# Who writes the low halves of the weights, where the convolution reads, who copies the S5 carries, and how rows are spread

## The chip, the cores and the metric

The kernel runs on one core of one Trainium2 chip. The metric is the device time of one launch in microseconds. The core has five engines with a queue each: PE (TensorE, with its weight loads shown as PEld), DVE (VectorE), ACT (ScalarE), POOL (GpSimd) and SP (SyncE, which here only starts DMAs). Each engine takes its instructions strictly in the order in which they stand in its queue and waits on semaphores for the others.

## The reference, cut to what matters

One inference step of a hybrid recurrent layer for 2,048 prompt tokens, 16 meta tokens and 8 short sample sequences of 8 tokens. All is float32.

```
h = rms_norm(x); proj = h @ w_in                      # 1024 -> 8,720 columns
A: q,k,v = silu(causal_conv4(qkv)); gated delta rule  # DeltaNet, 4 heads of 128
B: mLSTM with exponential gates                       # 4 heads of 128
C: S5: h[t] = lam*h[t-1] + B u[t], y = Re(C h) + d*u  # 32 groups, 64 complex states, then GLU
x = x + (sum_b sigmoid(gate_b) * (branch_b @ w_b)) @ w_out;  y = rms_norm(x)
```

`causal_conv4` is a convolution over the last four tokens with four taps per feature. Its input is the projected column block itself, and the last three columns of one stretch of tokens are carried to the next.

## The kernel before, in words

The tokens are cut into six blocks of 336, 384, 384, 384, 384 and 256 columns (`BLOCKS`; the first also holds the samples and the meta tokens). Activations lie feature-major: 128 features on the partitions, tokens along the row. A dense product (`product`) makes 128 output features for all tokens of a block and sums over 8 or 4 slices of 128 input features into one bank of PSUM, called `pd`; there are three such banks. Because PE gets its operands as rounded halves, every slice takes three matmuls: high weights by high activations, high weights by low activations, low weights by high activations.

The weights of four slices form a piece of 128x512 floats (`weights`): SP loads it (`w`), ACT casts it to the high half (`wh`), and a subtraction `w - wh` makes the low half (`wl`). A block needs 182 pieces and the program 1,092. The subtraction is given to DVE or to POOL by count: every second piece goes to POOL (`WPOOL = 2`), in the first block every fourth (`WPOOL0 = 4`). There are three buffers of `wh` and three of `wl`, so the halves of a piece can be written only when PE has finished the piece three earlier. A piece is 12 matmuls.

In each block the steps are issued in this order: `rows` (the per-token gates, a long chain of small DVE operations), `columns` (transposes of these rows on PE and exponentials), four S5 projections and four S5 scans (`s5_scan`), then the projections of q, k, v for DeltaNet (`dn_proj`) and mLSTM (`ml_proj`) and the recurrences and outputs by the list `PLAN`. A scheduler turns that order, with priorities, into the order of each engine's queue; the loads, casts and subtractions of weights have a higher priority (`WPRIO`) than what is issued around them. So the order is written nowhere by hand.

`dn_proj` copies the product from `pd` to a buffer `raw` in SBUF (ACT), puts the three carried columns in front of it (POOL), multiplies by the last tap (ACT, `cacc`), adds the three other taps on DVE from shifted views of `raw`, and saves the last three columns (POOL, buffer `cbuf`). `s5_scan` copies the carried state of four columns into the scan's first column (DVE), scans with DVE, combines with DVE and POOL, and copies the state at the end out again (DVE). `spread` brings a row of the gates into all partitions by a matmul of 32 rows of ones with 32 rows of `rx`; `rx` has three such groups of 32 rows.

Most arithmetic goes through helpers, so that in the profile L185 is any `tensor_tensor`, L193 any `scalar_tensor_tensor`, L196 any matmul, L179 a copy, L182 an activation, and the tiles tell which is which.

Of the kernel before, what the change touches and what calls it, by code (L numbers as in the profile page):

```python
# [17 lines left out]
D = 1024  # L18
# [9 lines left out]
# Prompt tiles of 128 tokens per block; the first block also has the tile of samples and meta tokens.  # L28
# [7 lines left out]
WPOOL, WPOOL0 = 2, 4  # L36
WB = (4, 3, 3)
UNITS = 12
# Order of the steps of the first block and of the others: projections of q, k, v (d, m), recurrences, outputs.
PLAN0 = ("m8 m7 R m6 m10 m1 m0 m9 m2 m4 m5 d4 m3 d5 m11 M d0 d3 d2 S d7 d8 d9 d10 d1 d6 pre inv d11 N X1 D "  # L40
         "F X2 Ud E X0 Um").split()
PLAN = ("d0 d1 m1 m0 m2 m3 d6 d2 d10 d3 m4 m7 m6 d7 d4 d5 m5 d8 pre d9 m9 d11 m11 m10 m8 M F N inv D X2 "
        "X1 E X0").split()

# Buffers of temporaries: floats of a partition, and how many.
# [17 lines left out]
# Column blocks of the input projection, in the order in which the host lays them out.  # L63
CB_S5U, CB_DN, CB_ML, CB_MLO, CB_MLZ, CB_S5Z, CB_DNZ, CB_GATE = 0, 4, 16, 28, 32, 36, 40, 44

# Columns of the array of vectors.
V_NW, V_TAP, V_BG, V_DNN, V_MLN, V_S5D, V_BGLU, V_FN, V_RB, V_AL, V_LDT, V_LR, V_LI, NV = (
    0, 8, 56, 80, 81, 82, 86, 90, 98, 99, 100, 116, 132, 148)
# Columns of the array of constants.
# [34 lines left out]
class Kernel:  # L104
# [36 lines left out]
    def temp(self, shape, tag, dt=F32):  # L141
        """A tile of a set of buffers that several steps share."""
# [14 lines left out]
    def pair(self, w, name):  # L157
        """Two tiles of the four heads, the second of width w, in one unit."""
        u = self.unit([P, 4 * P + 4 * w], name=name)
        return u[:, 0:4 * P].rearrange("p (h n) -> p h n", h=4), u[:, 4 * P:].rearrange("p (h n) -> p h n", h=4)  # L160
# [41 lines left out]
    def rsqrt(self, out, x, shape, also_sqrt=None):  # L202
        """out = 1/sqrt(x) on a small tile of positive floats: a first guess from their bits, three Newton steps."""
# [13 lines left out]
    def weights(self, src, k0):  # L217
# [3 lines left out]
        with self.tc.high_priority(offset=WPRIO if self.wn > 1 else 5500):  # L221
            self.nc.sync.dma_start(w, src[:, k0:k0 + 4])
            self.A.copy(h, w)  # L223
            self.wn += 1
            pool = WPOOL if self.b else WPOOL0
            self.tt(self.G if pool and self.wn % pool == 0 else self.V, l, w, h, OP.subtract)
        return h, l

    def product(self, src, nk, xh, xl, T):
        t = self.pd.tile([P, 512], F32, name=self.name("pd"), tag="pd")  # L230
        o = t[:, :T]
        for k in range(nk):
# [4 lines left out]
            self.mm(o, l[:, k % 4], xh(k), start=False, stop=k == nk - 1)  # L237
        return o

    def proj(self, cb):  # L240
        return self.product(self.I["wi"][cb], 8, lambda k: self.xh[k // 4][:, k % 4, :],
                            lambda k: self.xl[k // 4][:, k % 4, :], self.T)

# [1 line left out]
    def setup(self):  # L245
# [14 lines left out]
        self.G.memset(self.ones, 1.0)  # L260
        self.halfv = self.const([P, NV])
        self.ts(self.V, self.halfv, self.vec, 0.5, OP.mult)
        c = self.small([P, 8], "setup")
        # the row groups' bias with its sign, and the rows' factor of softplus
# [19 lines left out]
    def block(self, b):  # L284
# [20 lines left out]
        # (first column, sequences, their length): chunks over which decays are summed  # L305
        self.segs = ([(0, 8, 8), (NS, 1, NM)] if self.first else []) + [(self.p0, BLOCKS[b], P)]

    def norm(self):
        """xn^T = x^T * norm_w * rstd, as two exact halves."""
# [12 lines left out]
        if self.first:  # L322
            # x^T * norm_w in halves, for the products that need not wait for rstd
# [37 lines left out]
    def rstd_row(self, acc):  # L361
        """1/rms of every token, in every partition of a row, from squares summed over k."""
# [16 lines left out]
    def bc(self, src, c0, ns, L, p0, p1, at):  # L379
        """[p, ns, L]: of each sequence its column `at`, repeated."""  # L380
# [6 lines left out]
    def rows(self):  # L387
# [11 lines left out]
        # softplus(u) = max(u, 0) + 2 artanh(e / (2 + e)), e = exp(-|u|)  # L399
# [17 lines left out]
        # cumulative sums by chunk: G in rows 0.., b in rows 32..  # L417
# [10 lines left out]
        # running maximum; M[:, 1 + t] is m after token t, M[:, 0] the block's first m  # L428
# [26 lines left out]
        # rows that go to all partitions: G; b - m; b + m(chunk start) - m  # L455
# [12 lines left out]
        # rows that become columns: G, G_last - G | ig - b, its state weight, -m | beta  # L468
# [1046 lines left out]
```

## Time and profile before

| what | value |
|---|---|
| time, median of 3 runs | 2888.38 us (2888.12 to 2891.21) |
| span of the profiled execution | 2881.7 us |
| what lies around that span, by the median | 6.7 us |
| PE, matmuls | 2695.2 us, 94% |
| DVE | 2005.7 us, 70% |
| POOL | 1463.6 us, 51% |
| ACT | 1237.3 us, 43% |

The profile is of one execution; its own total time is not listed apart from its span, so that 6.7 us of start and end are taken as the difference to the median. Busy times are sums over the whole span. A stage in which PE is busy all the time is set by PE; in the other stages one looks at what PE waits for. The granted clock is the share of full speed that TensorE's clock had in a stretch.

### The profile page before, as it was taken

Reading aid. Unit: us, or ns where it says so; the run is one execution under the profiler, and the core shown is the slowest. Engines: PE = TensorE matmul, PEld = TensorE weight load, DVE = VectorE, ACT = ScalarE, POOL = GpSimd, SP = SyncE. Lnnn points to the kernel's source line nnn. Section 1 sums busy time; section 2 is a strip of 40 time slices with the busy share of each in tenths; the row PEclk is TensorE's granted clock in tenths of the full one; section 3 lists DMA queues with packets and bytes.
Section 4 is the critical chain, followed back from the end, with each engine's and each line's share of the span. In section 5 each row is a group of like instructions: output and inputs, shape, how many; then the busy total and the mean of one; then the engine's idle time right before and its main releaser. Section 6 shows DMA issues by size and latency. Waiting matters only on the chain.

```text
span 2881.7 us, 49911 instructions
## 1 busy us (share of the span) xinstructions
PE 2695.2 (94%) x17416; PEld 2585.0 (90%) x17416; DVE 2005.7 (70%) x4030; ACT 1237.3 (43%) x2639; POOL 1463.6 (51%) x1545
## 2 busy tenths in 40 slices
PE   6898999998999999999998999999999999989897
PEld 5798888887999989899998989999989999978897
DVE  8789756789753488884458888345988734688854
ACT  4353334434533443443453453345335334444444
POOL 8853444355434545543464553445455345455555
PEclk9999999999999999999999999999999999998999
DMA  5544547544333455433345533345543434564544
GB/s 154 162 152 147 154 149 219 171 154 126 98 112 107 149 168 159 121 110 105 112 155 166 163 103 119 99 122 164 168 147 102 122 98 135 159 192 124 152 144 151
DMA packets 303292, 404.26 MB, mean 140 GB/s; under 512 B 109472, under 2 KB 138912, under 8 KB 303040
## 3 DMA queue, kind: packets, MB, share of 16 engines
q1 hardware_dynamic: 283248, 374.73, 43.0%
q10 hardware_dynamic: 19792, 26.34, 2.7%
q8 instruction: 137, 2.24, 0.3%
q14 instruction: 115, 0.94, 0.1%
HBM read 369.42 MB, written 31.53 MB: 139 GB/s over the span
## 4 chain that ended last, share of the span: by engine, by line
PE 40%; DVE 16%; issue 3%; DMA 3%; ACT 2%; POOL 1%; SPq 0%; DVEq 0%; ACTq 0%; POOLq 0%
PE pd L196 32%; PE pr L196 5%; DVE wl L185 2%; DVE cacc L193 2%; DVE s5a L1196 2%; PE s L196 1%; DVE invT L185 1%; DVE s5a L185 1%; DVE invU L185 1%; PE pr L200 1%; ACT wh L223 1%; DMA ox<-in_xt_dram 1%; DVE h L193 1%; POOL wl L185 1%; DVE nacc L185 1%
## 5 line engine op out<-in xcount | busy, mean ns | idle before, releaser
L185 POOL TENSOR_TENSOR wl<-w,wh 128x512 fp32r<-128x512 f32 x500 | 690.2, 1381 | 882.2 <-ACT wh L223 789.4
L196 PE MATMUL pd<-xh,wl 128*128 128x384 f32 (+2 forms) x3272 | 1083.9, 332 | 57.8 <-DVE wl L185 49.1
L223 ACT CAST wh<-w 128x512 fp32r<-128x512 f32 x1092 | 672.8, 618 | 1059.8 <-PE pd L196 742.1
L196 PE MATMUL pd<-xh,wh 128*128 128x384 f32 (+2 forms) x3272 | 1079.1, 330 | 6.5 <-ACT wh L223 5.3
L196 PE MATMUL pd<-xl,wh 128*128 128x384 f32 (+2 forms) x3272 | 1076.8, 329 | 3.5 <-DVE xl L185 3.5
L185 DVE TENSOR_TENSOR wl<-w,wh 128x512 fp32r<-128x512 f32 x592 | 469.8, 794 | 361.3 <-ACT wh L223 335.3
L196 PEld LDWEIGHTS pd<-xh,wl 128*128 128x128 f32 x3272 | 625.8, 192 | 84.0 <-DVE wl L185 63.5
L196 PEld LDWEIGHTS pd<-xh,wh 128*128 128x128 f32 x3272 | 627.9, 192 | 13.0 <-ACT wh L223 7.2
L196 PEld LDWEIGHTS pd<-xl,wh 128*128 128x128 f32 x3272 | 627.3, 192 | 9.0 <-DVE xl L185 4.7
L193 DVE SCALAR_TENSOR_TENSOR cacc<-raw,c,cacc 128x384 f32<-128x384 f32 (+2 forms) x252 | 171.0, 694 | 4.6 <-ACT cacc L182 2.5
L185 POOL TENSOR_TENSOR macc<-macc,mt 128x384 f32<-128x384 f32 (+2 forms) x96 | 106.2, 1107 | 56.8 <-DVE mt L193 54.9
L196 PE MATMUL pd<-mh,wl 128*128 128x384 f32 (+2 forms) x384 | 125.3, 329 | 5.3 <-POOL wl L185 4.2
L196 PE MATMUL pd<-mh,wh 128*128 128x384 f32 (+2 forms) x384 | 125.9, 330 | 3.6 <-DVE h L193 3.2
L196 PE MATMUL pd<-ml,wh 128*128 128x384 f32 (+2 forms) x384 | 124.4, 326 | 0.0
L193 DVE SCALAR_TENSOR_TENSOR mt<-mt,pd 128x384 f32<-128x384 f32 (+2 forms) x96 | 50.0, 521 | 96.3 <-PE pd L196 94.5
L185 POOL TENSOR_TENSOR s5a<-s5a,s5a 128x384 f32<-128x384 f32 (+2 forms) x72 | 82.6, 1156 | 66.5 <-DVE s5a L185 60.7
L185 DVE TENSOR_TENSOR invT<-invP,invU 48x31 f32<-48x31 f32 (+25 forms) x186 | 100.4, 540 | 10.4 <-DMA invP<-scrp 6.3
L1196 DVE TENSOR_TENSOR_SCAN s5a<-s5R,s5a,s5a 128x96 f32<-128x96 f32 (+2 forms) x192 | 97.5, 566 | 2.8 <-POOL s5a L185 2.7
L182 ACT ACTIVATE raw<-cacc 128x384 f32<-128x384 f32 (+2 forms) x72 | 35.9, 499 | 147.5 <-DVE cacc L193 136.5
L185 POOL TENSOR_TENSOR s5a<-s5a,s5t 128x384 f32<-128x384 f32 (+2 forms) x48 | 66.5, 1386 | 45.8 <-DVE s5a L1196 27.7
L196 PE MATMUL s<-s5U,s5w 128*128 128x96 f32 (+2 forms) x576 | 85.5, 278 | 3.4 <-DMA s5U<-us 2.3
L185 DVE TENSOR_TENSOR nacc<-nacc,nsq 128x384 f32<-128x384 f32 (+2 forms) x84 | 68.5, 816 | 28.4 <-ACT nsq L182 26.5
(396 smaller groups left out, 4744.5 us busy)
## 6 DMA issues: line engine op xcount, KB each, us to landing
w<-in_wi_dram SPq DMA_DIRECT2D x816, 256.0 KB
w<-in_wb_dram SPq DMA_DIRECT2D x144, 256.0 KB
s5w<-s5w SPq DMA_DIRECT2D x120, 256.0 KB
w<-in_wo_dram SPq DMA_DIRECT2D x96, 256.0 KB
s5t<-s5p SPq DMA_DIRECT2D x48, 192.0 KB
w<-in_wg_dram SPq DMA_DIRECT2D x24, 256.0 KB
xt<-in_xt_dram SPq DMA_DIRECT2D x32, 192.0 KB
ox<-in_xt_dram ACTq DMA_DIRECT2D x32, 192.0 KB
```

What stands on the lines that cost most here:

```text
L182: return self.A.activation(out, in_, f, **k)
L185: return eng.tensor_tensor(out, a, b, op=op)
L193: return self.V.scalar_tensor_tensor(out, a, s, b, op0=op0, op1=op1)
L196: return self.E.matmul(out, lhsT, rhs, start=start, stop=stop, **k)
L200: return self.E.transpose(out, in_, self.ident[:n, :n])
L223: self.A.copy(h, w)
L1196: V.tensor_tensor_scan(g[:, a, 1:1 + m], self.s5R[:, 4 * f + a:4 * f + a + 1].to_broadcast([P, m]), x[:, a, 0:m], g[:, a, 0:1], OP.mult, O ...
```

## The change

Four edits. All 1,092 subtractions go to DVE. In all blocks but the first the convolution reads the product in its bank of PSUM: the product is put 16 columns to the right, ACT writes the three carried columns just in front of it, and DVE's three taps read shifted views of the bank; the buffer `raw` then only takes the tanh. ACT also saves the last three columns, in all blocks. The six small copies of each S5 scan go from DVE to ACT. `spread` uses 96 rows of `rx` with a selector that is one in one group of 32 rows and zero elsewhere. The names `u0` to `s3` in `PLAN` issue the S5 steps in the place where they stood before.

```diff
 def weights(self, src, k0):
     ...
             self.wn += 1
-            pool = WPOOL if self.b else WPOOL0
-            self.tt(self.G if pool and self.wn % pool == 0 else self.V, l, w, h, OP.subtract)
+            self.tt(self.V, l, w, h, OP.subtract)
-    def product(self, src, nk, xh, xl, T):
+    def product(self, src, nk, xh, xl, T, lead=None):
         t = self.pd.tile([P, 512], F32, name=self.name("pd"), tag="pd")
         o = t[:, :T]
+        if lead is not None:
+            o = t[:, 16:16 + T]
     ...
+        if lead is not None:
+
+            self.A.copy(t[:, 13:16], lead)
+            self.lead = t
         return o
 def setup(self):
     ...
+        self.sel = self.const([P, 4], F32R, name="sel")
+        t = self.sel.bitcast(F32)
+        self.G.memset(t, 0.0)
+        for g in range(3):
+            self.G.memset(t[32 * g:32 * g + 32, g:g + 1], 1.0)
 def spread(self, i, g):
     ...
-        self.mm(p, self.onesr[32 * g:32 * g + 32], self.rx[32 * g:32 * g + 32, i, 0:4 * n])
+        self.mm(p, self.sel[0:96, g:g + 1].to_broadcast([96, P]), self.rx[0:96, i, 0:4 * n])
 def dn_proj(self, n):
     ...
-        ps = self.proj(CB_DN + n)
+        ps = self.proj(CB_DN + n, None if self.first else self.cbuf[b % 2][:, n])
     ...
+            self.A.copy(raw[:, so + 3:so + 3 + T - NS], ps[:, NS:T])
+            parts.append((acc[:, NS:T], lambda j: raw[:, so + j:so + j + T - NS]))
         else:
-            self.copy(self.G, raw[:, 0:3], self.cbuf[b % 2][:, n])
-        p1 = NS if self.first else 0
-        self.A.copy(raw[:, so + 3:so + 3 + T - p1], ps[:, p1:T])
-        parts.append((acc[:, p1:T], lambda j: raw[:, so + j:so + j + T - p1]))
-        self.copy(self.G, self.cbuf[(b + 1) % 2][:, n], raw[:, so + T - p1:so + T - p1 + 3])
+            parts.append((acc[:, :T], lambda j, t=self.lead: t[:, 13 + j:13 + j + T]))
+        self.A.copy(self.cbuf[(b + 1) % 2][:, n], ps[:, T - 3:T])
 def s5_scan(self, f):
     ...
-            self.copy(V, g[:, :, 0:1], car[:, j, ps4][:, :, None])
+            A.copy(g[:, :, 0:1], car[:, j, ps4][:, :, None])
     ...
-            self.copy(V, t[:, :, c0:c0 + 1], car[:, j, ps4][:, :, None])
+            A.copy(t[:, :, c0:c0 + 1], car[:, j, ps4][:, :, None])
     ...
-            self.copy(V, carn[:, j, ps4][:, :, None], hs[j][:, :, c0 + m:c0 + m + 1])
+            A.copy(carn[:, j, ps4][:, :, None], hs[j][:, :, c0 + m:c0 + m + 1])
```

What this does to the queues is shown at two places of the fourth block (a block of 384 columns). The first is DVE's queue around the S5 scan of the first column block, between one low half `wl` and the next that DVE makes. Before, with `s5a` and `s5car` the S5 buffers, `rx` the spread rows, `dn` and `cacc` the convolution of DeltaNet:

```order
L185 TENSOR_TENSOR wl_17514<-w_17512,wh_17513 128x512
L179 COPY s5a_3508_17050<-s5car_813 128x4
L190 TENSOR_SCALAR cx_16840<-cx_16840 128x3x4
L189 TENSOR_SCALAR eg_16845<-eg_16845 128x12
L185 TENSOR_TENSOR rx_16853<-rE_16812,c_92 96x512 x3
L179 COPY s5a_3509_17051<-s5car_813 128x4
L193 SCALAR_TENSOR_TENSOR dn_17384<-raw_17374,cacc_17375 128x384
L193 SCALAR_TENSOR_TENSOR cacc_17424<-raw_17423,c_100,cacc_17424 128x384
L1196 SCALAR_TENSOR_TENSOR s5a_3508_17050<-s5R_251,s5a_3508_17050,s5a_3504_17046 128x96 x4
L185 TENSOR_TENSOR wl_17552<-w_17550,wh_17551 128x512
```

The two low halves are those of the 18th and the 21st piece of the block; the two between them are POOL's. The same place after the change (lines are one lower in the helpers):

```order
L184 TENSOR_TENSOR wl_17531<-w_17529,wh_17530 128x512
L1205 SCALAR_TENSOR_TENSOR s5a_3509_17031<-s5R_256,s5a_3509_17031,s5a_3505_17027 128x96
L184 TENSOR_TENSOR rx_16834<-rE_16793,c_92 96x512 x3
L1205 SCALAR_TENSOR_TENSOR s5a_3509_17031<-s5R_256,s5a_3509_17031,s5a_3505_17027 128x96 x2
L189 TENSOR_SCALAR cx_16821<-cx_16821 128x3x4
L1205 SCALAR_TENSOR_TENSOR s5a_3509_17031<-s5R_256,s5a_3509_17031,s5a_3505_17027 128x96
L188 TENSOR_SCALAR eg_16826<-eg_16826 128x12
L1205 SCALAR_TENSOR_TENSOR s5a_3510_17032<-s5R_256,s5a_3510_17032,s5a_3506_17028 128x96 x4
L192 SCALAR_TENSOR_TENSOR dn_17364<-raw_17356,cacc_17357 128x384
L192 SCALAR_TENSOR_TENSOR dn_17364<-raw_17404,cacc_17405 128x384
L184 TENSOR_TENSOR wl_17549<-w_17547,wh_17548 128x512
```

Now the two low halves are neighbours (the 21st and 22nd piece), the small copies are gone, and all eight scans of this column block stand between them. The second place is ACT's queue at the first DeltaNet projections behind the scans. Before, with `raw<-pd` the copy of the product and `raw<-cacc` the tanh:

```order
L223 CAST wh_17686<-w_17685 128x512
L548 COPY raw_17624<-pd_17587 128x384
L182 ACTIVATE cacc_17625<-pd_17587,c_100 128x384
L223 CAST wh_17704<-w_17703 128x512
L182 ACTIVATE raw_17624<-cacc_17625 128x384
```

After, from the S5 carries (`s5car<-s5a`) to the same projection, with `pd<-c` and `c<-pd` the carried columns of the convolution:

```order
L1220 COPY s5car_817<-s5a_3505_17027 128x4
L222 CAST wh_17616<-w_17615 128x512
L181 ACTIVATE ml_17413<-pd_17528 128x384
L1220 COPY s5car_817<-s5a_3506_17028 128x4
L222 CAST wh_17634<-w_17633 128x512
L222 CAST wh_17663<-w_17662 128x512
L240 COPY pd_17566<-c_116 128x3
L559 COPY c_115<-pd_17566 128x3
L181 ACTIVATE cacc_17605<-pd_17566,c_105 128x384
L1243 COPY s5y_17072<-s_3511_17059 128x384
L181 ACTIVATE raw_17604<-cacc_17605 128x384
```

The copy of 384 columns is gone, two copies of three columns stand in its place, and copies of the S5 carries, which wait for the end of a scan, stand ahead of casts.

## Rows read from the trace of the kernel before

**Rows 1.** The page: busy time of each engine over the span.
```profile
PE 2695.2 (94%) x17416; PEld 2585.0 (90%) x17416; DVE 2005.7 (70%) x4030; ACT 1237.3 (43%) x2639; POOL 1463.6 (51%) x1545
```

**Rows 2.** The view of the cores: span and mean granted TensorE clock.
```profile
core 0: 2881.7 us, clock 0.973
```

**Rows 3.** Waits of PE, whole span: us in total, times, longest us.
```profile
PE pd L196 <- DVE wl L185: 56.7, 57, 4.6
PE pd L196 <- POOL wl L185: 13.2, 12, 2.2
PE pd L196 <- DVE macc L193: 3.8, 3, 2.5
```

**Rows 4.** Stretches of the fourth block: length, busy time by engine, granted clock, DMA.
```profile
1550.30:1595.00 44.70, 38.27 (x223) 37.09 (x222) 37.57 (x62) 16.79 (x36) 21.23 (x20) 0.96 0.46 142
1685.70:1736.30 50.60, 46.99 (x290) 44.93 (x289) 40.58 (x75) 28.61 (x75) 29.95 (x25) 0.93 0.33 92
1799.60:1971.80 172.20, 172.20 (x1163) 168.47 (x1163) 66.28 (x118) 74.41 (x155) 82.19 (x80) 1.00 0.40 123
sum 487.40, PE 465.64 PEld 451.33 DVE 328.26 ACT 209.53 POOL 238.36; mean PE 51.74 PEld 50.15 DVE 36.47 ACT 23.28 POOL 26.48
```

**Rows 5.** Waits of PE in that block, 1518 to 1800 us.
```profile
PE pd L196 <- DVE wl L185: 8.2, 8, 2.2
PE pr L200 <- ACT ml L182: 3.6, 1, 3.6
PE pr L200 <- DVE rX L193: 2.5, 1, 2.5
PE s L196 <- POOL s5a L185: 2.3, 2, 1.6
PE s L196 <- DVE s5a L185: 1.6, 2, 1.1
```

**Rows 6.** DVE by line and shape: busy us, mean ns, idle before.
```profile
L185 DVE TENSOR_TENSOR wl<-w,wh 128x512 fp32r<-128x512 f32 x592 | 469.8, 794 | 361.3 <-ACT wh L223 335.3 <-DMA ys<-s5y 9.5 <-DMA xt<-in_xt_dram 7.4
L193 DVE SCALAR_TENSOR_TENSOR cacc<-raw,c,cacc 128x384 f32<-128x384 f32 x144 | 112.7, 784 | 3.4 <-ACT cacc L182 2.1
L1196 DVE TENSOR_TENSOR_SCAN s5a<-s5R,s5a,s5a 128x96 f32<-128x96 f32 x128 | 70.7, 611 | 2.8 <-POOL s5a L185 2.7
L179 DVE COPY s5a<-s5car 128x4 f32<-128x4 f32 x96 | 44.6, 481 | 0.0
L193 DVE SCALAR_TENSOR_TENSOR h<-h,c,pr 128x384 f32<-128x384 f32 x32 | 17.1, 607 | 0.1
L179 DVE COPY s5car<-s5a 128x4 f32<-128x4 f32 x48 | 16.2, 356 | 4.8 <-POOL s5a L185 4.7
L185 DVE TENSOR_TENSOR mldd<-pr,mldd 128x512 f32<-128x512 f32 x16 | 11.0, 687 | 6.0 <-PE pr L196 4.2 <-ACT mldd L182 1.8
```

**Rows 7.** POOL by line and shape.
```profile
L185 POOL TENSOR_TENSOR wl<-w,wh 128x512 fp32r<-128x512 f32 x500 | 690.2, 1381 | 882.2 <-ACT wh L223 789.4 <-DVE nacc L185 21.5 <-DVE wl L185 18.6
```

**Rows 8.** ACT by line and shape.
```profile
L223 ACT CAST wh<-w 128x512 fp32r<-128x512 f32 x1092 | 672.8, 618 | 1059.8 <-PE pd L196 742.1 <-issue 96.3 <-POOL wl L185 56.8
L548 ACT COPY raw<-pd 128x384 f32<-128x384 f32 x48 | 22.7, 472 | 3.1 <-DVE dn L193 1.8 <-PE pd L196 1.3
L178 ACT COPY U<-pr 32x128 f32<-32x128 f32 x32 | 8.2, 256 | 7.0 <-PE pr L196 6.7
```

**Rows 9.** Timeline of the second block: start, us, engine, operation.
```profile
601.24 1.69 POOL L185 TENSOR_TENSOR wl<-w,wh 128x512 fp32r<-128x512 f32 x1
...
601.32 0.33 PE L196 MATMUL pd<-xh,wh 128*128 128x384 f32 x1
...
601.49 0.33 PE L196 MATMUL pd<-xl,wh 128*128 128x384 f32 x1
...
601.79 1.15 DVE L179 COPY s5car<-s5a 128x4 f32<-128x4 f32 x1
...
602.86 0.68 DVE L185 TENSOR_TENSOR wl<-w,wh 128x512 fp32r<-128x512 f32 x1
```

More of the change, by code (lines that the diff above doesn't have):

```diff
@@ L35 @@
 SPRIO = 1500
-WPOOL, WPOOL0 = 2, 4
 WB = (4, 3, 3)
@@ L41 @@
          "F X2 Ud E X0 Um").split()
-PLAN = ("d0 d1 m1 m0 m2 m3 d6 d2 d10 d3 m4 m7 m6 d7 d4 d5 m5 d8 pre d9 m9 d11 m11 m10 m8 M F N inv D X2 "
+PLAN = ("u0 u1 u2 u3 s0 s1 s2 s3 d0 d1 m1 m0 m2 m3 d6 d2 d10 d3 m4 m7 m6 d7 d4 d5 m5 d8 pre d9 m9 d11 m11 m10 m8 M F N inv D X2 "
         "X1 E X0").split()
@@ L237, in product, with proj @@
             self.mm(o, l[:, k % 4], xh(k), start=False, stop=k == nk - 1)
+        if lead is not None:
+            self.A.copy(t[:, 13:16], lead)
+            self.lead = t
         return o
-    def proj(self, cb):
+    def proj(self, cb, lead=None):
         return self.product(self.I["wi"][cb], 8, lambda k: self.xh[k // 4][:, k % 4, :],
-                            lambda k: self.xl[k // 4][:, k % 4, :], self.T)
+                            lambda k: self.xl[k // 4][:, k % 4, :], self.T, lead)
     def setup(self):
@@ L1331, in plan @@
             add(self.columns)
-        for f in range(4):
-            add(self.s5_proj, f)
         if self.first:
+            for f in range(4):
+                add(self.s5_proj, f)
             add(self.normed)
-        if not self.first:
-            for f in range(4):
-                add(self.s5_scan, f)
         for w in PLAN0 if self.first else PLAN:
@@ L1362, in plan @@
                     add(self.s5_scan, f)
+            if w[0] == "u":
+                add(self.s5_proj, int(w[1:]))
+            if w[0] == "s":
+                add(self.s5_scan, int(w[1:]))
             if w == "Um":
```

## The prediction

> **What bounds the kernel now.** I began with the page [rows 1]: PE runs matmuls for 2695.2 of 2881.7 us [rows 2], so at most 186.5 us of the span is PE idle, and no edit removes a matmul. [...] The stretches show where: in the fourth block, of 487.4 us with 465.6 us of PE [rows 4], the mixing stage of 172.2 us has PE busy throughout at a clock of 1.00, while the stretch of the S5 scans has 6.4 us of PE idle in 44.7 us at 0.96, and that of the first mLSTM tiles 3.6 us in 50.6 us at 0.93 [rows 4]. Low clock comes where PE has been idle. [...]
>
> Those waits [rows 5]: low halves made by DVE 8.2 us, mLSTM's eviction 3.6, the gate rows 2.5, and the S5 combination 2.3 on POOL and 1.6 on DVE. Over the whole span PE waited 56.7 us for low halves of DVE and 13.2 us for those of POOL [rows 3]. DVE is thus the engine that PE waits for, though it is busy for only 70% [rows 1]: in the S5 stretch it is at 37.6 of 44.7 us, in the mixing stage at 66.3 of 172.2 [rows 4].
>
> **Why DVE is late.** The timeline shows DVE held up by POOL [rows 9]. A copy of four columns starts at 601.79 and takes 1.15 us; it ends at 602.94, with POOL's low half (601.24 + 1.69 = 602.93). The low half that DVE makes right after takes 0.68 us. The groups show the same as averages [rows 6]: a low half takes 794 ns, and `mldd`, an operation of the same length with one input in PSUM, 687; a tap of the convolution from SBUF takes 784, and `h`, of the same form with one input in PSUM, 607; four columns take 481 and 356 ns.
>
> **The change, part by part.**
>
> *Low halves.* POOL loses 500 operations and 690 us [rows 7]. DVE gets 500 x 0.687 = 344 us if none is held up by what POOL still does, 500 x 0.794 = 397 us if as many are as now; I take 0.72, between them and nearer the lower end since POOL's work is halved: 360 us.
>
> *Carries.* 96 + 48 copies leave DVE: 44.6 + 16.2 = 61 us [rows 6]. On ACT the trace has no copy of four columns; the nearest is 256 ns for 128 columns [rows 8], so 144 x 0.26 = 37 us is the upper end and nothing the lower (ACT is idle 57% [rows 1]). ACT's casts stand behind these copies, and the last two of a scan wait for POOL. The cover is the lead of the casts: ACT waited 742 us for PE to free a buffer of high halves [rows 8]. Without it each blocked copy would cost PE its own wait, up to 1.6 us (the longest of POOL's [rows 5]) for 48 copies. I take nothing.
>
> *Convolution.* 144 taps of 384 columns go from 784 to about 607 ns (the row of the same form [rows 6]): 25 us off DVE; the narrower blocks are not counted. Lower end: no gain, if reading the second input from SBUF were the slow part. ACT drops 48 copies of 472 ns [rows 8] and gets 132 small ones, about even. POOL drops as many. But the bank stays taken until DVE has done three taps, some 3 x 0.607 = 1.8 us plus its queue, where ACT freed it before. PE's next use of that bank comes two products later, 2 x 24 matmuls at 0.17 us (601.32 to 601.49 [rows 9]) = 8.2 us. Other products hold their bank for DVE already, and PE waited 3.8 us in all for the main one, `macc` [rows 3]. I take nothing, with the upper end as a rival.
>
> [...]
>
> *Spreading.* 51 matmuls keep their 512 columns. Bounds are nothing and one tenth of a us each, 5 us; I take nothing, the weights being one column repeated.
>
> *What DVE's queue gains and loses.* DVE: 2006 + 360 - 61 - 25 - 592 x 0.107/2 (half of what its own low halves lose to POOL now) = 2248 us, 78%. So DVE gets more work as a sum, in stages that differ: in the S5 stretch the copies leave and POOL's hold is halved, in the mixing stage there is room for all of it.
>
> *What the order adds.* There are three buffers of low halves, so between one low half and the next PE has three pieces of 12 x 0.17 = 2.04 us in hand, 6.1 us. Before, POOL made pieces between two of DVE's, and the gap could be longer. At the place in DVE's queue shown above there stand after the change eight scans (8 x 0.611 = 4.9 us), three `rx` and the low half (4 x 0.687 = 2.7), two `dn` (2 x 0.607 = 1.2), together 8.9 us [rows 6]: PE waits up to 2.8 us, about 1 if the scans are no longer held up. Going through the fourth block's queue in this way at unhindered prices I find six gaps longer than PE's three pieces, by some 8 us together, against two gaps by some 2 us together before.
>
> **The sum.** In a block like the fourth: low halves, six gaps at 1.8 us (1.4 unhindered, and a little for POOL) = 10.8 us for 8.2: +2.6. The S5 combination no longer stands behind POOL's low halves of 1.38 us [rows 7] nor behind held-up copies: 3.9 to 0.7, -3.2. Gate rows and mLSTM's eviction, chains of small operations that each can be held for a us: 6.1 to 3.1, -3.0. Together -3.6 us of waits, x 1.42 = -5.1 us, for five blocks -25.6. The first block keeps its convolution in SBUF and POOL's S5 set-up; it only gets 45 more low halves at DVE's rate of waits, 45 x 56.7/592 x 1.42 = +6.1. So the span goes to 2881.7 - 25.6 + 6.1 = 2862.2, and with the 6.7 us around it (median 2888.38 less the span) to 2869 us, 0.7% less. About 0.2% is what a measurement of this kernel can tell from no change.
>
> **The rivals.**
>
> *The hold was the whole trouble (faster still).* If a quarter of all PE idle goes, 186.5/4 x 1.42 = 66 us, the time is 2822. For it: low halves on DVE are 16% dearer than the like operation [rows 6], and such holds fall just where PE waits. Against: the six gaps, which remain without any POOL.
>
> *One queue for all low halves (slower).* DVE waits in its queue for every cast, and the low halves that POOL made, of which PE missed 13.2 us, are missed as often as DVE's: 500 x 56.7/592 - 13.2 = +34.7 us of waits, x 1.42 = +49 us: 2938. For it: DVE's wait is the largest row, POOL's is small [rows 3], and DVE's sum rises to 78%. Against: the held-up operations. It decides from the point where PE waits 13.7/5 = 2.7 us more for low halves in each block than I forecast, 13.5 in place of 10.8. [...]
>
> *The banks (slower).* If every third of the 60 moved convolutions costs PE 1 us: 20 x 1.42 = 28, so 2897. The row of `macc` [rows 3] speaks against it.
>
> *Nothing moves.* PE's waits are lumps in the order, and who makes a low half hardly matters: 2885 to 2891.
>
> **Chances.** Forecast 0.40 (its own range 2845 to 2882), faster still 0.18, one queue 0.22, banks 0.05, nothing 0.15. Faster by over 0.2%: 0.57; within: 0.16; slower: 0.27. The range from 2815 to 2930 leaves out the far ends of the second and third case.
>
> **What would show it.** Right: DVE's low halves near 0.72 us, DVE near 78% and POOL near 27% (1463.6 - 690 over the span); PE's waits for POOL's S5 operation near nothing; the S5 stretch shorter and at a higher clock; PE's waits for low halves at 60 to 75 us in all. The first step is wrong if low halves stay near 0.79 us, the order's step if waits for low halves fall below 40 us, and the whole if they pass 90 or if PE waits for taps of the convolution.

## The result and the profile after

The changed kernel takes 2820.03 us (median of 4 runs, 2815.57 to 2822.66) against 2889.80 us of before on the same chip: a ratio of 0.9759 with a 95% interval from 0.9744 to 0.9775, 2.4% faster. The forecast was 0.7% faster. The profiled execution has a span of 2813.8 us.

The page's busy line and the cores view of the changed kernel answer to [rows 1] and [rows 2]:

```profile
PE 2657.2 (94%) x17416; PEld 2579.1 (92%) x17416; DVE 2049.5 (73%) x4386; ACT 1256.8 (45%) x2855; POOL 759.0 (27%) x917
```

```profile
core 0: 2813.8 us, clock 0.975
```

DVE took over 500 low halves and is still busy for only 44 us more than before, 2049.5 us, where 2248 was forecast. PE is busy for 38.0 us less. PE's idle time went from 186.5 to 156.6 us. So the 67.9 us that the span lost are 38.0 of busy time and 29.9 of waiting.

PE's waits over the whole span (us in total, times, longest us) answer to [rows 3]:

```profile
PE pd L195 <- DVE wl L184: 21.6, 28, 2.7
PE pd L195 <- DVE cacc L192: 16.8, 6, 4.8
PE pr L195 <- POOL va L895: 15.4, 3, 5.2
...
PE s L195 <- POOL s5a L184: 8.3, 5, 2.5
```

Low halves cost PE 21.6 us, where those of DVE and POOL had cost 69.9 [rows 3]. Among the larger rows, `cacc`, the convolution's taps that now hold a bank of PSUM, is new, and POOL's `va` is up from 1.9. Three more grew: DVE's `xl` from 3.5 to 9.4 us and a wait for nothing that the profile shows from 0.8 to 9.2, each now one wait in the first block, and ACT's `xh` from 0.3 to 9.0. POOL's S5 operation, which was to fall to near nothing, stands at 8.3 where it had 7.9; that on DVE (5.8 before) is gone.

The stretches of the fourth block (columns as in [rows 4]) that answer to the three shown there, and PE's waits in that block (1501 to 1776 us), which answer to [rows 5]:

```profile
1531.70:1573.90 42.20, 37.12 (x216) 36.00 (x216) 33.03 (x61) 17.03 (x47) 11.43 (x7) 0.96 0.47 144
...
1657.00:1708.90 51.90, 47.09 (x290) 46.85 (x291) 41.79 (x86) 28.86 (x75) 21.69 (x20) 0.93 0.29 85
...
1768.70:1940.80 172.10, 172.10 (x1165) 168.58 (x1164) 89.18 (x158) 72.39 (x152) 41.02 (x43) 1.00 0.39 120
...
sum 475.60, PE 461.55 PEld 452.71 DVE 336.65 ACT 212.56 POOL 110.92; mean PE 51.28 PEld 50.30 DVE 37.41 ACT 23.62 POOL 12.32
```

```profile
PE pr L195 <- POOL va L895: 5.2, 1, 5.2
PE s L195 <- POOL s5a L184: 2.5, 1, 2.5
PE pd L195 <- DVE cacc L192: 2.0, 1, 2.0
PE pd L195 <- DVE wl L184: 1.5, 5, 0.6
```

The block takes 475.6 us in place of 487.4. The stretch of the S5 scans went from 44.7 to 42.2 us at the same clock of 0.96; that of the first mLSTM tiles got longer, 50.6 to 51.9, with POOL's `va` where the gate rows and `ml` had been waited for; the mixing stage is as long as it was. PE waits 1.5 us for low halves in the whole block, where 8.2 was measured before and 10.8 forecast. The wait for `va` is for a memset of four columns that takes 0.10 us: it stands in POOL's queue behind three `P`, an `s5g` and an `ml`, 6.6 us in a row.

```profile
1655.14 3.68 POOL L184 TENSOR_TENSOR P<-P,dnx 128x512 f32<-128x512 f32 x3 [2.99 <-DVE dnx L184]
...
1661.70 0.10 POOL L895 MEMSET va<- 128x4 f32 x1
```

DVE's operations by line and shape answer to [rows 6]:

```profile
L184 DVE TENSOR_TENSOR wl<-w,wh 128x512 fp32r<-128x512 f32 x1092 | 812.7, 746 | 407.1 <-ACT wh L222 393.4 <-DMA ys<-s5y 4.1 <-PE pr L195 3.9
L192 DVE SCALAR_TENSOR_TENSOR cacc<-pd,c,cacc 128x384 f32<-128x384 f32 x144 | 87.0, 609 | 2.5 <-ACT cacc L181 1.5
L1205 DVE TENSOR_TENSOR_SCAN s5a<-s5R,s5a,s5a 128x96 f32<-128x96 f32 x128 | 56.2, 495 | 0.3 <-POOL s5a L184 0.3
L184 DVE TENSOR_TENSOR nacc<-nacc,nsq 128x384 f32<-128x384 f32 x56 | 38.8, 693 | 6.5 <-ACT nsq L181 5.5
...
L192 DVE SCALAR_TENSOR_TENSOR h<-h,c,pr 128x384 f32<-128x384 f32 x32 | 17.1, 606 | 1.1 <-PE pr L195 1.1
```

The low half went from 794 to 746 ns, the scan from 611 to 495. `nacc`, which no edit touches, took 870 ns before and takes 693: both its inputs are in SBUF. `h<-h,c,pr`, with one input in PSUM, stands where it stood, 607 and 606. So operations that DVE reads twice from SBUF got cheaper beside the low halves, though not all of them: `s5a<-s5a,s5t` of 384 columns went from 770 to 910 ns. The averages hide how the hold falls. The view of the tile `wl` gives the shortest, the median and the longest low half of DVE in ns, before and after:

```profile
L185 DVE TENSOR_TENSOR wl<-w,wh x592: 655/692/1778, 5.7 to 2862.0; 128x512 fp32r<-128x512 f32 x198
...
L184 DVE TENSOR_TENSOR wl<-w,wh x1092: 621/692/1784, 5.6 to 2797.1; 128x512 fp32r<-128x512 f32 x182
```

The median is 692 ns in both. The hold is a long wait of a minority, and that minority became smaller: 117 of 592 took over 800 ns before, 124 of 1,092 do now.

### The profile page after: what moved, and what is told of

Same layout as the page of the kernel before. It is cut to its first block, busy times and chain, and to the rows that moved or that the text cites. A ratio compares the mean times of both kernels' runs of the same rounds, so it can differ in the third digit from the quotient of the medians.

```text
span 2813.8 us, 49701 instructions
## 1 busy us (share of the span) xinstructions
PE 2657.2 (94%) x17416; PEld 2579.1 (92%) x17416; DVE 2049.5 (73%) x4386; ACT 1256.8 (45%) x2855; POOL 759.0 (27%) x917
## 4 chain that ended last, share of the span: by engine, by line
PE 80%; DVE 11%; POOL 3%; DMA 2%; issue 2%; ACT 1%; SPq 0%; DVEq 0%; ACTq 0%; POOLq 0%
PE pd L195 66%; PE pr L195 9%; PE s L195 3%; DVE wl L184 2%; PE pr L199 2%; DVE s5a L1205 1%; POOL s5a L184 1%; DMA ox<-in_xt_dram 1%; DVE h L192 1%; DVE s5a L184 1%; DVE cacc L192 1%; DMA w<-in_wi_dram 1%; POOL P L184 1%; POOL s5xy L184 0%; ACT xh L357 0%
## 5 line engine op out<-in xcount | busy, mean ns | idle before, releaser
L222 ACT CAST wh<-w 128x512 fp32r<-128x512 f32 x1092 | 673.9, 619 | 990.5 <-PE pd L195 828.5
L184 DVE TENSOR_TENSOR wl<-w,wh 128x512 fp32r<-128x512 f32 x1092 | 812.7, 746 | 407.1 <-ACT wh L222 393.4
L195 PE MATMUL pd<-xh,wh 128*128 128x384 f32 (+2 forms) x3272 | 1078.7, 330 | 28.5 <-DVE cacc L192 16.8
L184 POOL TENSOR_TENSOR macc<-macc,mt 128x384 f32<-128x384 f32 (+2 forms) x96 | 124.7, 1299 | 389.0 <-DVE mt L192 382.3
L184 POOL TENSOR_TENSOR s5a<-s5a,s5a 128x384 f32<-128x384 f32 (+2 forms) x72 | 76.9, 1075 | 555.4 <-DVE s5a L184 522.6
L192 DVE SCALAR_TENSOR_TENSOR cacc<-pd,c,cacc 128x384 f32<-128x384 f32 (+1 forms) x180 | 103.9, 582 | 2.8 <-ACT cacc L181 1.5
L178 POOL COPY U<-UC 32x128 f32<-32x128 f32 x68 | 21.7, 337 | 290.5 <-DMA UC<-scru 289.2
L195 PEld LDWEIGHTS s<-s5U,s5w 128*128 128x128 f32 x576 | 79.3, 197 | 16.0 <-issue 15.5
L195 PEld LDWEIGHTS pd<-mh,wh 128*128 128x128 f32 x384 | 74.2, 193 | 14.6 <-ACT xh L357 13.0
L181 ACT ACTIVATE mt<-pd,c 128x384 f32<-128x384 f32 (+2 forms) x144 | 79.4, 551 | 0.4
L195 PEld LDWEIGHTS pd<-mh,wl 128*128 128x128 f32 x384 | 74.2, 193 | 5.9 <-DVE wl L184 5.8
```

What stands on the lines that cost most here:

```text
L178: return eng.tensor_copy(out, in_)
L181: return self.A.activation(out, in_, f, **k)
L184: return eng.tensor_tensor(out, a, b, op=op)
L192: return self.V.scalar_tensor_tensor(out, a, s, b, op0=op0, op1=op1)
L195: return self.E.matmul(out, lhsT, rhs, start=start, stop=stop, **k)
```

## The experiments

All ratios are to the kernel before on the same chip, with a 95% interval; us worked out from a ratio use 2888. Four runs make one edit each in the kernel before, four undo one edit in the changed kernel, one makes two edits, three load POOL with work that nothing reads, and four change the order of the queues.

**The low halves alone.** In the kernel before:

```diff
-WPOOL, WPOOL0 = 2, 4
+WPOOL, WPOOL0 = 0, 0
```

> The kernel before with only the low halves all on DVE. Theory (POOL's low halves hold up DVE, and that is most of what PE waits for): PE's waits for low halves fall from 70 us to 35 or less, other DVE operations with two inputs in SBUF get 10% shorter, 30 to 45 us less, ratio 0.985 to 0.990. Rival (one queue for all low halves is a load that only the other edits make room for): waits for low halves rise above 70 us and the ratio is 1.000 to 1.017.

Measured: 0.9788 [0.9772, 0.9803], 61 us less: nearly the whole result, and more than the theory's 30 to 45 us. Its busy line and PE's wait for low halves:

```profile
PE 2679.3 (95%) x17416; PEld 2581.5 (91%) x17416; DVE 2062.5 (73%) x4530; ACT 1249.1 (44%) x2639; POOL 813.9 (29%) x1045
```

```profile
PE pd L196 <- DVE wl L185: 32.4, 40, 2.7
```

With the span of 2829.4 us, PE idle fell from 186.5 to 150.1 us. DVE's time outside the low halves fell from 1535.9 (2005.7 - 469.8) to 1261.1 us (2062.5 - 801.4), though it does the same work: 275 us less. The largest single part is in no row shown ahead of the prediction: `invT<-invP,invU`, a step of DeltaNet's triangular inverse, fell from 100.4 to 61.8 us. The 96 small copies of [rows 6] hardly moved, from 481 to 461 ns, so most of their length was not the hold by POOL's low halves; the 48 others went from 356 to 200. The profiled execution, at 2831.2 us, is the slowest of its four (median 2824.65).

**The low halves undone.** The changed kernel with every second low half (every fourth in the first block) on POOL again:

```diff
-            self.tt(self.V, l, w, h, OP.subtract)
+            pool = 2 if self.b else 4
+            self.tt(self.G if self.wn % pool == 0 else self.V, l, w, h, OP.subtract)
```

> The changed kernel with POOL's share of the low halves given back (every second, every fourth in the first block); the other three edits stay. Theory (the low halves are nearly all of the change): all but the 8 us of the spreading is lost or more, since carries and convolution alone cost 0.2 to 0.4%: ratio 0.995 to 1.005. Rival (the edits help each other): ratio 0.985 to 0.992.

Measured: 0.9932 [0.9915, 0.9948], 50 us of the 70 given back, with 799 ns for a low half and PE's waits for low halves at 47.5 us for DVE's and 15.1 for POOL's. The ratio lies between the theory's range and the rival's. The three other edits together are worth 0.7%.

**What the low halves gave: work moved, hold, or POOL's queue.** Two kernels keep all low halves on DVE and load POOL again. The first lets POOL overwrite the raw piece with `w - w`, which nothing reads, behind the low half. The second writes it with three memsets instead, so that POOL is as busy and waits at the same places, but reads nothing.

```diff
             self.tt(self.V, l, w, h, OP.subtract)
+            if self.wn % (2 if self.b else 4) == 0:
+                self.tt(self.G, w, w, w, OP.subtract)      # the first kernel
+                for _ in range(3): self.G.memset(w, 0.0)   # the second kernel, in its place
```

> The changed kernel, and POOL overwrites the raw weights of every second piece (every fourth in the first block) with w - w once both halves are made; nothing reads them. Theory (what the change gave back is the hold: a POOL operation that reads SBUF keeps DVE out): DVE's low halves go from 746 to 800 ns or more, other DVE operations lengthen as before the change, and 40 to 70 us of the gain are lost, though DVE still makes all low halves: ratio 0.990 to 1.002 to the kernel before. Rival (the gain is that a low half no longer stands in POOL's queue, with POOL's longer operation and the wait behind other work): DVE's prices may rise but the time stays within 10 us of the changed kernel, ratio 0.976 to 0.980.

> As d_pool, but with three memsets of the raw weights in place of the subtraction: POOL is about as long busy (3 x 0.53 = 1.6 us) and reads nothing from SBUF. Theory (the hold needs POOL to read SBUF): DVE's low halves stay near 746 ns and the time within 10 us of the changed kernel, ratio 0.976 to 0.980. Rival (any work of POOL of this length delays, through its queue or through writes): as d_pool.

Measured: 1.0122 [1.0103, 1.014] for the first, 0.9922 [0.9905, 0.9939] for the second, both above their theory's range: the second keeps the prices of the low halves, as it was expected to, but not the time. The groups of the low half and of POOL's added work, the busy line, and PE's wait for low halves, of the kernel that reads:

```profile
L184 DVE TENSOR_TENSOR wl<-w,wh 128x512 fp32r<-128x512 f32 x1092 | 860.6, 791 | 342.6 <-ACT wh L222 337.1 <-PE pd L195 1.4
...
L184 POOL TENSOR_TENSOR w<-w 128x512 f32<-128x512 f32 x500 | 585.8, 1172 | 1011.3 <-DVE wl L184 648.4 <-issue 242.9 <-DVE ff L189 19.3
```

```profile
PE 2702.6 (92%) x17416; PEld 2607.7 (89%) x17416; DVE 2219.2 (76%) x4386; ACT 1251.4 (43%) x2855; POOL 1354.0 (46%) x1417
```

```profile
PE pd L195 <- DVE wl L184: 45.4, 54, 3.0
```

and of the kernel that only writes:

```profile
L184 DVE TENSOR_TENSOR wl<-w,wh 128x512 fp32r<-128x512 f32 x1092 | 811.7, 745 | 448.2 <-ACT wh L222 435.1 <-PE pd L195 4.8 <-DMA s5U<-us 1.4
L227 POOL MEMSET w<- 128x512 f32 x1500 | 790.9, 528 | 897.3 <-DVE wl L184 808.7 <-issue 14.6 <-DMA out_yt_dram<-h 10.2
```

```profile
PE 2680.7 (94%) x17416; PEld 2594.0 (91%) x17416; DVE 2052.5 (72%) x4386; ACT 1251.8 (44%) x2855; POOL 1529.4 (53%) x2417
```

```profile
PE pd L195 <- DVE wl L184: 19.2, 29, 2.1
```

POOL is busier in the second kernel, 1529.4 against 1354.0 us, yet the low half falls from 791 to 745 ns, DVE's sum from 2219.2 to 2052.5 us and PE's wait from 45.4 to 19.2 us. So in these two kernels it is POOL's reading of SBUF that holds DVE, by 46 ns in the average low half, not POOL's being busy.

The four kernels make a chain with the other edits fixed. From the undone low halves (0.9932) to POOL reading (1.0122) DVE gets 500 low halves more while POOL goes on holding it, and POOL's added work now waits for DVE and keeps the raw piece longer: +55 us for all of this. From there to the memsets (0.9922) only the reading ends: -58 us. From there to the changed kernel (0.9759) POOL's added work and its waiting end: -47 us.

**POOL busy, without the waiting.** The last step has two parts: POOL's time, and its queue standing still for a piece (808.7 us of waiting for `wl` in the row of the memsets), with the raw piece held longer. This kernel gives POOL the time alone, on a small tile that nothing reads:

```diff
+        self.dump = self.const([P, 8])
     ...
+            if self.wn % (2 if self.b else 4) == 0:
+                for _ in range(14):
+                    self.G.memset(self.dump, 0.0)
```

> The changed kernel, and POOL also writes 14 memsets of 8 columns of a tile that nobody reads, for every second piece (fourth in the first block); they wait for no other engine. Theory (the 46 us that the memsets of the raw weights cost came from POOL's queue standing still until a low half is made, and from the raw buffer held longer, not from POOL's busy time): at most 15 us more than the changed kernel, ratio 0.976 to 0.981. Rival (POOL's busy time by itself delays the S5 and mLSTM operations behind it): 30 us or more, ratio 0.986 or higher.

Measured: 0.9826 [0.9811, 0.984], between theory and rival, POOL busy for 1460.8 us. So POOL's time makes about 19 us of the 47, and some 28 are left for the waiting or the longer hold of the raw piece, which no run tells apart.

**The spreading.** Alone in the kernel before, and undone in the changed one:

```diff
-        self.mm(p, self.onesr[32 * g:32 * g + 32], self.rx[32 * g:32 * g + 32, i, 0:4 * n])
+        self.mm(p, self.sel[0:96, g:g + 1].to_broadcast([96, P]), self.rx[0:96, i, 0:4 * n])
```

> The kernel before with only the spreading by 96 rows. Theory (a matmul of 32 rows costs PE about 0.39 us more between its neighbours than one of 96 rows, read from the two timelines): 51 x 0.39 = 20 us less, ratio 0.993, and the pitch around a spread like after's. Rival (PE's spreads lie beside waits, and my forecast of at most 5 us holds): ratio 0.998 to 1.000.

> The changed kernel with the spreading by 32 rows again. Theory (a matmul of 32 rows costs PE 0.39 us more among its neighbours; with fewer waits around, most of 51 x 0.39 = 20 us is paid): 12 to 20 us more than the changed kernel, ratio 0.980 to 0.983. Rival (the 8 us that the edit alone gave are all it is worth): ratio 0.977 to 0.979.

Measured: 0.9972 [0.996, 0.9985] alone and 0.9819 [0.9798, 0.984] undone, so 8 us and 17 us; 8 is far less than the theory's 20. On top of the low halves (the kernel with both, below) it is 9 us, from 0.9788 to 0.9757. PE's busy time moves by 17.1 us (2695.2 to 2678.1) and by 19.3 us (2657.2 to 2676.5). The timeline shows why, first of the kernel before, then of the changed one:

```profile
1703.89 0.34 PE L196 MATMUL pd<-yh,wl 128*128 128x384 f32 x1
1704.16 0.49 PE L196 MATMUL pr<-rx,c 32*128 32x512 f32 x1
1704.58 0.44 PE L196 MATMUL pd<-yh,wh 128*128 128x384 f32 x1
1704.86 0.33 PE L196 MATMUL pd<-xh,wh 128*128 128x384 f32 x1
```

```profile
1646.06 0.34 PE L195 MATMUL pd<-xl,wh 128*128 128x384 f32 x1
1646.23 0.40 PE L195 MATMUL pr<-rx,sel 96*128 96x512 f32 x1
1646.47 0.34 PE L195 MATMUL pd<-xh,wl 128*128 128x384 f32 x1
1646.64 0.34 PE L195 MATMUL pd<-xh,wh 128*128 128x384 f32 x1
```

With 32 rows, three steps of PE take 0.97 us (1703.89 to 1704.86); with 96 rows, 0.58 us (1646.06 to 1646.64). At this place the matmul of 32 rows costs 0.39 us more: the neighbours start late before and behind it. Over all 51 places the median of the three steps is 0.89 us in the kernel before and 0.58 in the changed one, so 0.31 us each and 16 us in all, which goes better with PE's busy time than 51 x 0.39 = 20. That the rows make the difference, and not the other weights, is not shown apart. Alone, some 10 us turned into waits: the idle time of PE rose from 186.5 to 197.0 us.

**The convolution and the carries.** Each alone in the kernel before, and each undone in the changed one:

```diff
-            self.copy(V, g[:, :, 0:1], car[:, j, ps4][:, :, None])    # the carries, three such lines
+            A.copy(g[:, :, 0:1], car[:, j, ps4][:, :, None])
     ...
-        parts.append((acc[:, p1:T], lambda j: raw[:, so + j:so + j + T - p1]))    # the convolution
+            parts.append((acc[:, :T], lambda j, t=self.lead: t[:, 13 + j:13 + j + T]))
```

> The kernel before with only the convolution read from PSUM. Theory (taps go from 784 to about 607 ns, 25 us less of DVE in the first half of the blocks, part of it on the path): 0 to 12 us less, ratio 0.996 to 1.000. Rival (the bank that is held longer costs PE more than the taps give): ratio 1.002 to 1.006 and waits of PE for taps of the convolution.

> The kernel before with only the S5 carries on ACT. Theory (61 us of held-up copies leave DVE in the stretch of the S5 scans, where PE idles 5 to 6 us a block): 5 to 12 us less, ratio 0.996 to 0.998. Rival (ACT's casts stand behind copies that wait for POOL, whose low halves are still in front): same or slower, ratio 1.000 to 1.005, and more waits of PE for high halves.

> The changed kernel with the convolution read from SBUF again. Theory (once POOL is free the taps from SBUF are hardly held up, 627 against 609 ns, and the bank is freed earlier): 0 to 10 us less than the changed kernel, ratio 0.972 to 0.976. Rival (DVE is short of room, and the 25 us of taps count): 5 to 15 us more, ratio 0.978 to 0.981.

> The changed kernel with the S5 carries on DVE again. Theory (on DVE they no longer meet POOL often, on ACT they wait for POOL in front of casts): within 5 us of the changed kernel or up to 8 us less, ratio 0.973 to 0.978. Rival (the held-up copies matter still): 5 to 12 us more, ratio 0.978 to 0.980.

Measured: the convolution 1.0023 [1.0012, 1.0034] alone, 0.9832 [0.9815, 0.9849] undone; the carries 1.0043 [1.0029, 1.0058] alone, 0.9806 [0.9787, 0.9824] undone. Alone, both fall in the rival's range; undone, both cost as much as the rival's range or a little more. Each alone shows a wait of PE's that goes with it, for the taps and for ACT's casts (5.9 us in 7 waits before):

```profile
PE pd L196 <- DVE cacc L193: 12.3, 13, 2.2
```

```profile
PE pd L196 <- ACT wh L223: 21.7, 15, 4.4
```

**Low halves and spreading together**, convolution and carries as before (the diffs of those two in one kernel):

> The kernel before with the low halves on DVE and the spreading by 96 rows, convolution and carries as before. Theory (these two edits are the whole gain; the other two, which alone cost 0.2 and 0.4%, add nothing): 2805 to 2822 us, ratio 0.971 to 0.976, as fast as the changed kernel or faster. Rival (once DVE makes all low halves it needs the room that the other two edits give): 2824 us or more, ratio 0.978 or more.

Measured: 0.9757 [0.9737, 0.9778], 2820.58 us: as fast as the changed kernel without the other two edits. In it a tap from SBUF takes

```profile
L193 DVE SCALAR_TENSOR_TENSOR cacc<-raw,c,cacc 128x384 f32<-128x384 f32 x144 | 89.6, 627 | 3.9 <-ACT cacc L182 3.1
```

so 627 ns where it took 784 with POOL's low halves [rows 6], and 609 from PSUM. In this kernel most of what the convolution was to gain came with the low halves. With the convolution alone undone in the changed kernel, which differs from this one by the carries on ACT, it did not:

```profile
L192 DVE SCALAR_TENSOR_TENSOR cacc<-raw,c,cacc 128x384 f32<-128x384 f32 x144 | 100.1, 699 | 3.9 <-ACT cacc L181 3.2
```

There POOL makes no low halves either, and the tap averages 699 ns (its median is 612, as in the kernel with two edits), so that reading from PSUM takes 13 us off DVE. PE's wait for low halves is higher in the kernel with two edits, 34.3 us, and its wait for taps is not among the larger rows.

**The order of the queues.** The convolution and the carries cost when made alone, gain when undone singly, and are worth nothing together. The four last runs change the priority of loads, casts and low halves, which changes the order of the queues and no work: twice in the changed kernel, and once in each of the two with one edit undone.

```diff
-WPRIO = 400
+WPRIO = 360    # 440 in the three others
```

> The changed kernel with the priority of loads, casts and low halves at 360 in place of 400: the same instructions in a slightly other order of the queues. Theory (the half per cents of the small edits are order): the ratio to before moves by 0.4% or more from 0.9759, either way, so 0.972 or 0.980. Rival (the order is worth little and the edits need each other): within 0.2%, 0.974 to 0.978.

> The changed kernel with that priority at 440, a second sample of the order. Theory (order): 0.4% or more from 0.9759. Rival (edits need each other): 0.974 to 0.978, and the two samples of the order agree with each other.

> The changed kernel with the convolution undone and that priority at 440. Theory (order): anywhere from 0.974 to 0.984, unrelated to the 0.9832 at 400. Rival (edits need each other): 0.983 again, within 0.2%, and 0.7% above the run of the changed kernel at 440.

> The changed kernel with the carries undone and that priority at 440. Theory (order): anywhere from 0.974 to 0.984, unrelated to the 0.9806 at 400. Rival (edits need each other): 0.981 again, within 0.2%, and 0.5% above the run of the changed kernel at 440.

Measured: the changed kernel 0.9804 [0.9791, 0.9818] at 360 and 0.9779 [0.9765, 0.9792] at 440, beside 0.9759 at 400; the convolution undone 0.9807 [0.9794, 0.982]; the carries undone 0.9781 [0.9765, 0.9796]. The order alone was worth up to 0.45%, 13 us, in these three samples: at 360 it moved the ratio by the theory's 0.4%, at 440 it stayed within the rival's 0.974 to 0.978. At 440 the carries make no difference (0.9781 and 0.9779) and the convolution 0.3%. So the half per cent of the carries did not come again in another order. The convolution lies within what the order gives, but costs in both orders when undone, and its SBUF tap averages 699 ns in both; whether it has a small gain of its own beside the carries on ACT stays open. The steps of 50 to 61 us on the low halves are about four times the order's, and the spreading is measured in PE's busy time, which the order moved by 2.2 and 6.0 us (2659.4 and 2663.2 beside 2657.2), against 15.5 to 19.3 for the spreading; the 19 us of POOL's time, and with them the 28 that are left, are no surer than the order's 13.

## Why the forecast fell short

The sign, the engine that PE waits for and the cause of its lateness were right; the size was not. The forecast had PE's idle time fall by 13.7 us and the span by 19.5; idle fell by 29.9 and the span by 67.9. Two steps failed most: the order, which was to cost 10.8 us of waits for low halves in a block like the fourth and cost 1.5, and the spreading, taken at nothing, which shortened PE's busy time by 15.5 to 19.3 us. The time came out at that of the rival "the hold was the whole trouble", 2822 us. Its cause was nearer, since the low halves alone gave 61 of its 66 us, but that the time was met to 2 us is in part luck: it had 46.6 us of PE's idle going where 29.9 went, and it did not count the spreading. Step by step:

- *Each us of PE idle is worth 1.42 us*: no run shows this factor of the sum and of the rivals, 1 + 78/186.5 with 78 us for (1 - 0.973) of the span. What came is near in size, but its reason is not shown. With the low halves alone, which leave PE's work as it is, idle fell by 36.4 and the span by 52.3 us: 1.44. The granted clock, though, is 0.973 in both traces, so (1 - 0.973) of the span went only from 78 to 76 us. PE's busy time fell by 15.9; what made the rest of it stays open. Between the kernel that reads and the one that only writes, the same ratio is 1.58 (59.8 us of span, 37.9 of idle).
- *Low halves at 0.72 us*: about right. 746 ns on average over all 1,092, 812.7 us in all, where the forecast's terms give 798 (592 x (0.794 - 0.0535) + 500 x 0.72).
- *DVE's sum, 2248 us*: wrong by 199 us. The term that was mis-sized is "half of what its own low halves lose to POOL": it gave relief to the low halves alone. The rows of the taps, the copies and the scan stood in [rows 6] as held operations, and their relief was left out: 23, 10 and 15 us with the low halves alone. The rest of the 275 us that DVE lost outside the low halves through this one edit lies in rows that the forecast did not look at, `invT` first.
- *What the order adds*: the step that failed. The six gaps were to cost 10.8 us a block, 1.5 came. In the gap shown, which was summed to 8.9 us, the price of a scan, 0.611 us, was itself an average with POOL's hold. The forecast put all six gaps at 8 us even at unhindered prices; they are not listed one by one, so what was wrong in the other five stays open. The gap shown ahead of the prediction, in the timeline of DVE in the changed kernel:

```profile
1540.87 0.69 DVE L184 TENSOR_TENSOR wl<-w,wh 128x512 fp32r<-128x512 f32 x1
1541.48 0.42 DVE L1205 TENSOR_TENSOR_SCAN s5a<-s5R,s5a,s5a 128x96 f32<-128x96 f32 x1
1541.81 1.86 DVE L184 TENSOR_TENSOR rx<-rE,c 96x512 fp32r<-96x512 f32 x3
1543.59 0.72 DVE L1205 TENSOR_TENSOR_SCAN s5a<-s5R,s5a,s5a 128x96 f32<-128x96 f32 x2
1544.23 0.14 DVE L189 TENSOR_SCALAR cx<-cx 128x12 f32<-128x12 f32 x1
1544.29 0.40 DVE L1205 TENSOR_TENSOR_SCAN s5a<-s5R,s5a,s5a 128x96 f32<-128x96 f32 x1
1544.61 0.14 DVE L188 TENSOR_SCALAR eg<-eg 128x12 f32<-128x12 f32 x1
1544.67 1.98 DVE L1205 TENSOR_TENSOR_SCAN s5a<-s5R,s5a,s5a 128x96 f32<-128x96 f32 x4
1546.57 1.00 DVE L192 SCALAR_TENSOR_TENSOR dn<-raw,cacc 128x384 f32<-128x384 f32 x2
1547.49 1.28 DVE L184 TENSOR_TENSOR wl<-w,wh 128x512 fp32r<-128x512 f32 x2
1548.69 1.02 DVE L184 TENSOR_TENSOR s5a<-s5a,s5t 128x384 f32<-128x384 f32 x2
1549.63 0.68 DVE L184 TENSOR_TENSOR wl<-w,wh 128x512 fp32r<-128x512 f32 x1
...
1553.42 0.69 DVE L184 TENSOR_TENSOR wl<-w,wh 128x512 fp32r<-128x512 f32 x1 [2.64 <-ACT wh L222]
```

  From the end of the first low half (1541.56) to that of the next (1548.13) it takes 6.6 us, not 8.9; the eight scans take 3.5 us (0.42 + 0.72 + 0.40 + 1.98), not 4.9. PE has 6.1 us of pieces in hand there, so by the forecast's rule it would wait 0.5 us, not 2.8 nor the "about 1" without the hold, and no wait for a low half in this block is longer than 0.6 us. Behind it DVE makes two at once and soon waits for ACT's casts (2.64 us in the last line): it is ahead. Waits for low halves of 60 to 75 us over the span were forecast, 21.6 came, and below 40 this step was to be called wrong. That idle fell by only 16 us more than forecast goes with the rows that grew elsewhere: `cacc`, `va`, `xl` and `xh`.
- *One queue for all low halves, slower*: nearer to a kernel that was not the changed one. Where POOL goes on reading, the step to all low halves on DVE costs 55 us, against the 49 that this rival worked out, and the kernel is slower than before (1.0122). The likeness is not proof of its cause: PE's waits for low halves are 45.4 us there, fewer than the 69.9 before, and POOL's waiting for DVE is in the 55 too. The gain of the changed kernel hung on what POOL does in the place of its low halves: with the reading it is gone, and with the memsets it is that of the undone low halves (0.9922 and 0.9932).
- *Nothing for POOL's side*: POOL's queue that stood still for casts (789.4 us [rows 7]) was not counted as a cost to others. As the memsets measure them, 47 us hang on POOL's time and its waiting, some 28 of them on the waiting or the longer hold of the raw piece.
- *S5 and the gate rows*: a part of the size forecast. In the fourth block S5 waits went from 3.9 to 2.5, not 0.7; gate rows and `ml` (6.1) are gone from the list, not halved, but 5.2 for `va` came in, at the same mLSTM tile and for POOL's queue. Over the span PE's wait for POOL's S5 operation did not fall (7.9 and 8.3), and the clock of the S5 stretch did not rise.
- *Carries at nothing*: in the changed kernel they give or cost nothing that stands out of the order. The bounds held: ACT's copies take 195 and 198 ns.

The rows of these copies, with the idle time of ACT ahead of them:

```profile
L1217 ACT COPY s5a<-s5car 128x4 f32<-128x4 f32 x48 | 9.5, 198 | 47.8 <-DVE s5a L1205 43.1 <-DVE s5a L178 2.0 <-DVE rs_t L192 1.3
...
L1220 ACT COPY s5car<-s5a 128x4 f32<-128x4 f32 x48 | 9.3, 195 | 70.4 <-POOL s5a L184 50.7 <-DVE s5a L184 17.2 <-POOL va L895 2.5
```

  ACT did stand still for them, 50.7 us for POOL's combination and 43.1 for the scan, and the lead of the casts covered it: ACT waited 828.5 us for PE to free a buffer of high halves, PE 4.5 us for casts. Without the other edits it did not: PE waited 21.7 us for casts.
- *Convolution, 25 us off DVE and no price for the bank*: the tap's price is as forecast, 609 against 607 ns, but without POOL's low halves the SBUF tap was already down to 627, or 699 with the carries on ACT. The bank cost 16.8 us of PE's waits in 6 lumps, where nothing was taken; that is near the 20 us of the rival "the banks", and waits for taps were named as a sign that the forecast as a whole is wrong. Beside the SBUF tap of the kernel with two edits the tap from PSUM is not dearer: 609 against 627 ns on average, 608 against 612 by the median of the 144.
- *Spreading within 5 us*: wrong. The bound of a tenth of a us each had no row behind it; the 32-row matmul stands in the timeline of before 0.27 us behind the start of its predecessor and 0.42 us ahead of the next, and could have been read there.
- *First block +6.1*: measured from its first matmul to that of the second block, 534.7 and 534.8 us; with the low halves alone 540.2, near the forecast. *Five equal blocks at -5.1*: the four middle ones lost 11.3, 12.6, 11.7 and 9.1 us, and the last, of 256 columns, 23.4. With the low halves alone the last lost 19.4 already; why it lost most was not tried.

## What to carry to other kernels

Where one engine holds up another, as POOL does DVE here, price every operation of the held engine without the hold, not only the one that moves. The nearest row of the same form with an input in PSUM came close to that price here (`mldd` 687 ns, `h` 607, against medians of 692 for the low half and 612 for the tap from SBUF), and an average over held ones is no lower bound (794 ns for the low half before, 746 after); where only a minority is held, the median of the group shows the price as well (692 ns for the low half in both kernels). The long queue of small operations in the gap shown took 6.6 us where the buffers cover 6.1, and no wait for a low half in its block was longer than 0.6 us; so an order is judged at those prices, and half a per cent between two orders (0.45% here) says nothing about an edit. Giving a second engine a share of the work can cost more than it takes off the first: here 61 us went when the first engine took it all. Here the hold is shown as a cause (58 us between reading and writing); what the second engine's own time and waiting cost, 47 us together, is shown only as a whole.

## What was not expected of the hardware

A matmul of 32 rows among matmuls of 128 rows cost more of PE's pitch than one of 96 rows with the same 512 columns: 0.89 against 0.58 us over three steps by the median of 51 places. With POOL's low halves a scan of 96 columns on DVE took 611 ns on average [rows 6], without them 490. POOL's reading took the average low half to 791 ns, POOL's memsets, with more busy time, left it at 745, and the median is 692 in both.
